# The opening of a two-layer decoder trunk on one core: loading the input ahead of the first weights, and reordering the first gate's products

## The chip, the core and the metric

The kernel runs on one core of one Trainium2 chip. The metric is the device time of one execution in microseconds (us). Four engines matter here: TensorE (PE, with its weight loads PEld beside it), VectorE (DVE), ScalarE (ACT) and GpSimd (POOL). SyncE (SP) issues nearly all transfers from memory.

## The reference

Two layers, each of a half-step SwiGLU block, a mixer of three attention groups, and another half-step SwiGLU block. The input x is 256 tokens by 1024 features, in float32; a SwiGLU block has 2816 hidden columns. What the change touches is the very first norm and the first gate and up products:

```python
def rms_norm(x, g):
    y = x * rsqrt(mean(x * x, axis=-1, keepdims=True) + 1e-6)
    return y * g

def swiglu(x, w_gate, w_up, w_down):
    return (silu(x @ w_gate) * (x @ w_up)) @ w_down

h = x
for l in range(2):
    h = h + 0.5 * swiglu(rms_norm(h, ffn1_norm[l]), ffn1_w_gate[l], ffn1_w_up[l], ffn1_w_down[l])
    h = h + hybrid_mixer(rms_norm(h, mix_norm[l]), ...)
    h = h + 0.5 * swiglu(rms_norm(h, ffn2_norm[l]), ffn2_w_gate[l], ffn2_w_up[l], ffn2_w_down[l])
```

## The kernel before

**Products in three parts.** Every float32 operand that goes through TensorE is split into a high part, rounded to the format that TensorE takes at full speed, and a low part, the residual. A product is then high x high plus high x low plus low x high. A weight tile `raw` of 1024 columns a partition (8 blocks of 128 rows by 128 output columns) is copied to `wh` (the class `Weights`, method `high`, L117, on ACT) and its residual goes to `wl` (method `low`, L121, on DVE). The normed input lies in one tile `xhl` whose two halves are the high part `norm.h` and the low part `norm.l`, side by side for each of its 8 blocks. So one **wide** product, 512 columns, multiplies `wh` with both halves at once, and one **narrow** product, 256 columns, adds `wl` times the high half. `proj` does eight wide and eight narrow products for one tile of 128 hidden columns.

**The norm.** x is loaded into `trunk` with tokens on the partitions. `Norm.turn` (L329) turns two blocks of it with four TensorE transposes into a PSUM bank of the tag `acc`. `Norm.high` (L318, ACT) scales a block by the norm's gain `gT` and writes the high part; `Norm.low` (L321, DVE) writes the residual. The division by the root mean square comes later, on the hidden values. The gains arrive as rows and are turned by `turn_gains` (L177 on TensorE, copied by DVE, L178).

**Order.** Nothing reorders instructions: each engine runs them as the program writes them down. Transfers go through SP's queue in the order of the calls. The first two weight tiles are loaded by hand in pieces: raw 0 holds the first two gate tiles (its first tile in two pieces of 256 KB, its second as one of 512 KB), raw 1 the first two up tiles (512 KB each). Until now the queue begins: x quarter 0, first half of the first gate tile, x quarter 1, second half of that tile, x quarters 2 and 3, the first up tile, the second gate tile, the second up tile. On ACT's own queue the identity matrix and the gains are loaded.

**The opening.** TensorE does seven products of ones (`WARM`), the transposes of x's quarter 0, the gains' transpose, and seven more products of ones. Then it goes through x by quarters: for the first gate tile it does three narrow products a block (`wh` with the high half, `wl` with the high half, `wh` with the low half), 24 in all, with the next quarters' transposes between them. The first gate tile is split by halves: `wh` by ACT (L1118) and `wl` by POOL (L1119). Only then does `ffn` run `proj` for the first up tile (`u0`), the second gate tile (`g1`), the second up tile (`u1`) and so on; in the first block the tiles g0, u0, g1, u1 stand in four PSUM banks of the tag `gu`. The squares for the mean (L344) follow on ACT, and their sum and root are formed during g1 and u1.

## Time and profile before

| | |
|---|---|
| median of 3 runs | 1041.45 us (1041.19 to 1041.46) |
| the profiled execution | 1041.75 us, with a span of 1039.8 us on the core |
| TensorE busy | 1034.6 us, granted clock 1.00 |
| DVE, ACT, POOL busy | 808.5, 594.9, 142.7 us |
| bytes moved | 181.70 MB, 175 GB/s on average |

In the lines of the profile an instruction group is named by its line in the kernel (L294 is the one line through which all products go), its engine, what it writes and reads, its shape and its count. In a timeline the first number is the start in us from the span's beginning and the second the time to the end of the group; a bracket tells how long the engine stood idle before it and what released it. A waits row gives the total, the count and the longest. A windows row gives a stretch, its length, the busy time of PE, PEld, DVE, ACT and POOL, the granted clock, the DMA engines' busy share and their GB/s. An issue row of a transfer ends with its size and the time from issue to landing.

### The profile page before, as it was taken

Reading aid. Unit: us, or ns where it says so; the run is one execution under the profiler, and the core shown is the slowest. Engines: PE = TensorE matmul, PEld = TensorE weight load, DVE = VectorE, ACT = ScalarE, POOL = GpSimd, SP = SyncE. Lnnn points to the kernel's source line nnn. Section 1 sums busy time; section 2 is a strip of 40 time slices with the busy share of each in tenths; the row PEclk is TensorE's granted clock in tenths of the full one; section 3 lists DMA queues with packets and bytes.
Section 4 is the critical chain, followed back from the end, with each engine's and each line's share of the span. In section 5 each row is a group of like instructions: output and inputs, shape, how many; then the busy total and the mean of one; then the engine's idle time right before and its main releaser. Section 6 shows DMA issues by size and latency. Waiting matters only on the chain.

```text
span 1039.8 us, 15145 instructions
## 1 busy us (share of the span) xinstructions
PE 1034.6 (100%) x5659; PEld 899.4 (86%) x5659; DVE 808.5 (78%) x1536; ACT 594.9 (57%) x1047; POOL 142.7 (14%) x173
## 2 busy tenths in 40 slices
PE   9999999999999999999999999999999999999998
PEld 8888888898888888888888888888988888888887
DVE  4997777789876887777788777777898768877775
ACT  6565555667754655555466555547667556555551
POOL 1003000167700000000000200002765000000000
PEclk9999999999999999999999999999999999999999
DMA  9675555555431374654646464555455214564631
GB/s 322 218 245 181 189 207 171 175 187 185 154 130 42 122 242 161 204 193 172 202 163 215 159 240 158 207 171 185 163 193 173 81 61 160 184 237 147 223 122 41
DMA packets 130905, 181.70 MB, mean 175 GB/s; under 512 B 7008, under 2 KB 104720, under 8 KB 130832
## 3 DMA queue, kind: packets, MB, share of 16 engines
q1 hardware_dynamic: 130656, 180.65, 51.0%
q8 instruction: 45, 0.74, 0.3%
q14 instruction: 28, 0.23, 0.1%
q10 hardware_dynamic: 176, 0.07, 0.0%
HBM read 179.67 MB, written 1.05 MB: 174 GB/s over the span
## 4 chain that ended last, share of the span: by engine, by line
PE 99%; DMA 1%; ACT 0%; SPq 0%; DVE 0%; issue 0%
PE ps_gu L294 66%; PE ps_acc L294 30%; PE ps_acc L329 1%; PE ps_gu L948 1%; PE ps_gu L1050 1%; DMA trunk<-in_x_dram 1%; PE ps_acc L649 0%; PE ps_acc L948 0%; PE ps_gu L981 0%; ACT wh L117 0%; SPq L91 0%; SPq L188 0%; PE ps_acc L355 0%; PE ps_acc L981 0%; DVE tmp L435 0%; DVE trunk L368 0%
## 5 line engine op out<-in xcount | busy, mean ns | idle before, releaser
L121 DVE TENSOR_TENSOR wl<-raw,wh 128x1024 fp32r<-128x1024 f32 (+2 forms) x343 | 416.6, 1220 | 29.2 <-ACT wh L117 29.0
L117 ACT CAST wh<-raw 128x1024 fp32r<-128x1024 f32 (+2 forms) x343 | 345.7, 1036 | 5.4 <-PE ps_gu L294 4.8
L294 PE MATMUL ps_gu<-xhl,wh 128*128 128x512 f32 (+1 forms) x1408 | 335.2, 389 | 0.2 <-DVE tmp L435 0.2
L294 PEld LDWEIGHTS ps_gu<-xhl,wh 128*128 128x128 f32 x1408 | 261.7, 188 | 53.2 <-DVE tmp L435 0.4
L294 PEld LDWEIGHTS ps_gu<-xhl,wl 128*128 128x128 f32 x1400 | 180.7, 191 | 7.2
L294 PE MATMUL ps_gu<-xhl,wl 128*128 128x256 f32 x1400 | 184.5, 283 | 0.0
L294 PE MATMUL ps_gu<-wh,xhl 128*128 128x512 f32 (+2 forms) x512 | 158.5, 379 | 0.0
L435 DVE TENSOR_TENSOR tmp<-ps_gu,tmp 128x256 f32<-128x256 f32 x175 | 72.5, 423 | 107.4 <-ACT tmp L434 107.2
L294 PE MATMUL ps_acc<-wh,hh 128*128 128x512 f32 (+1 forms) x352 | 137.7, 391 | 0.0
L294 PE MATMUL ps_acc<-wl,hh 128*128 128x512 f32 (+1 forms) x352 | 137.5, 391 | 0.0
L294 PE MATMUL ps_acc<-wh,hl 128*128 128x512 f32 (+1 forms) x352 | 136.5, 388 | 0.0
L434 ACT COPY tmp<-ps_gu 128x256 f32<-128x256 f32 x175 | 63.1, 371 | 93.9 <-PE ps_gu L294 93.8
L294 PEld LDWEIGHTS ps_gu<-wh,xhl 128*128 128x128 f32 x512 | 94.8, 188 | 14.5
L449 ACT CAST hh<-tmp 128x256 fp32r<-128x256 f32 x80 | 32.6, 407 | 119.9 <-DVE tmp L446 119.9
L294 PE MATMUL ps_gu<-wl,xhl 128*128 128x512 f32 (+2 forms) x256 | 95.7, 374 | 0.0
L305 POOL TENSOR_TENSOR y_n<-msq,minus_half 128x2 f32<-128x2 f32 x6 | 7.7, 1281 | 539.9 <-DVE msq L304 539.9
L441 ACT ACTIVATE tmp<-tmp 128x256 f32<-128x256 f32 x88 | 36.9, 419 | 77.8 <-DVE tmp L439 77.4
L294 PEld LDWEIGHTS ps_acc<-wh,hl 128*128 128x128 f32 x352 | 66.1, 188 | 14.0
L294 PEld LDWEIGHTS ps_acc<-wh,hh 128*128 128x128 f32 x352 | 66.4, 189 | 11.7
L294 PEld LDWEIGHTS ps_acc<-wl,hh 128*128 128x128 f32 x352 | 66.4, 189 | 11.4 <-DVE wl L121 0.7
L294 PEld LDWEIGHTS ps_gu<-wl,xhl 128*128 128x128 f32 x256 | 48.2, 188 | 6.6
L318 ACT ACTIVATE xhl<-ps_acc,gT 128x256 fp32r<-128x256 f32 x48 | 19.1, 475 | 37.2 <-PE ps_acc L329 37.1
(221 smaller groups left out, 1013.7 us busy)
## 6 DMA issues: line engine op xcount, KB each, us to landing
raw<-in_ffn_w_down_dram SPq DMA_DIRECT2D x44, 1024.0 KB, 4.9
raw<-in_ffn_w_gate_dram SPq DMA_DIRECT2D x43, 1024.0 KB, 6.7
raw<-in_ffn_w_up_dram SPq DMA_DIRECT2D x43, 1024.0 KB, 7.4
raw<-in_w_in_dram SPq DMA_DIRECT2D x24, 1024.0 KB, 5.0
raw<-in_w_out_dram SPq DMA_DIRECT2D x8, 1024.0 KB, 4.8
raw<-in_w_in_dram SPq DMA_DIRECT2D x4, 768.0 KB, 4.7
raw<-in_w_in_dram SPq DMA_DIRECT2D x4, 656.0 KB, 5.2
trunk<-in_x_dram SPq DMA_DIRECT2D x4, 256.0 KB, 4.7
```

What stands on the lines that cost most here:

```text
L117: self.nc.scalar.copy(hv, src)
L121: (engine or self.nc.vector).tensor_tensor(lv, self.srcs[self.n_low], hv.bitcast(F32), op=ALU.subtract)
L294: T.matmul(o, l, r, start=start, stop=stop, skip_group_check=True)
L305: G.tensor_tensor(y, dst, minus_half[:, :n], op=ALU.pow)
L318: A.activation(self.h[:, m], src, AF.Copy, scale=gT[:, self.col + m:self.col + m + 1])
L329: T.transpose(ps[:, i, t * P:(t + 1) * P], trunk[:, t, (2 * mp + i) * P:(2 * mp + i + 1) * P], ident)
L434: A.copy(o, ps[:, 1])
L435: V.tensor_tensor(o, ps[:, 0], o, op=ALU.add)
L441: A.activation(th, t_, AF.Tanh, scale=0.5)
L449: (V.tensor_copy if late else A.copy)(hh, t_)
L948: T.transpose(b[:, j * P:(j + 1) * P], pj[i][:, j * P:(j + 1) * P], ident)
L1050: T.transpose(b[:66, i * S + t * P:i * S + (t + 1) * P], src[t][:, 2 * hp_ + i, :], ident)
```

## The change

It has five parts, all in the opening:

- SP's queue begins with x: quarters 0 and 1, then quarters 2 and 3 as one transfer of 512 KB. The two halves of the first gate tile follow, then the first up tile as before.
- The gains are turned ahead of x's quarter 0 on TensorE. x's quarters are turned one after the other, with 2, 3, 0 and 4 products of ones behind them; no gate product stands between them.
- On ACT, six of x's eight blocks come ahead of the first half of the gate tile, two behind it. The second half of the gate tile's `wh` is copied by DVE, behind six of the eight residuals of x.
- The first gate tile is done with wide products, like all other tiles: eight wide ones, then the first up tile's eight wide ones, then the gate's eight narrow ones and the up's eight narrow ones.
- `ffn` takes over both banks, `g0` and `u0`, and starts with g1.

From g1 on, every engine's instructions stand in the same order as before.

```diff
-    def load_x(mp):
-        cols = slice(256 * mp, 256 * mp + 256)
+    def load_x(mp, n=1):
+        cols = slice(256 * mp, 256 * (mp + n))
...
-    for mp in range(1, 4):
-        if mp < 3:
-            W.load(0, mp - 1)
-        load_x(mp)
+    load_x(1)
+    load_x(2, 2)
+    W.load(0, 0)
+    W.load(0, 1)
     W.load(1, 0)
     W.load(0, 2)
     W.load(1, 1)
...
-        first = g0 is not None
         early = {}
         if first:
-            u0 = proj()
+            g0, u0 = first
             g1 = proj(norm.sums, 6)
...
-    g0 = bank("gu").rearrange("p (a b) -> p a b", a=2)
+    first = [bank("gu").rearrange("p (a b) -> p a b", a=2) for _ in range(2)]
     xT = []
 
-    def turn_x(mp):
-        xT.append(norm.turn(mp))
-
-    def gate(w, xs, ks):
-        for k in ks:
-            mm(g0[:, int(xs is norm.l)], w[:, k], xs[:, k], w is wh and xs is norm.h and k == 0,
-               xs is norm.l and k == KT - 1)
+    def warm_up(n):
+        for i in range(n):
+            mm(warm[:, P:2 * P], ones, ones, False, i == n - 1)
...
-    def split_gate(hf):
+    def split_gate(hf, copy):
         ks = slice(4 * hf, 4 * hf + 4)
-        A.copy(wh[:, ks], src[:, ks])
+        copy(wh[:, ks], src[:, ks])
         G.tensor_tensor(wl[:, ks], src[:, ks], wh[:, ks].bitcast(F32), op=ALU.subtract)
 
-    turn_x(0)
     turn_gains(0)
-    for i in range(WARM):
-        mm(warm[:, P:2 * P], ones, ones, False, i == WARM - 1)
-    split_gate(0)
-    first_norm(0)
-    turn_x(1)
-    split_gate(1)
-    for mp in range(4):
-        ks = range(2 * mp, 2 * mp + 2)
-        gate(wh, norm.h, ks)
-        if mp < 2:
-            turn_x(mp + 2)
-        if mp > 0:
-            gate(wl, norm.h, range(4) if mp == 1 else ks)
-        gate(wh, norm.l, ks)
-        if mp < 3:
-            first_norm(mp + 1)
+    for mp, n in enumerate((2, 3, 0, 4)):
+        xT.append(norm.turn(mp))
+        warm_up(n)
+    for mp in range(3):
+        first_norm(mp)
+    split_gate(0, A.copy)
+    split_gate(1, V.tensor_copy)
+    first_norm(3)
     W.low_done()
-    W.take()
+    ws = [W.take()]
     W.high()
     W.low()
     W.high()
     W.low()
+    ws.append(W.take())
+    for w, ps in zip(ws, first):
+        for k in range(KT):
+            mm(ps, w[0][:, k], norm.x[:, k], k == 0, False)
+    for w, ps in zip(ws, first):
+        for k in range(KT):
+            mm(ps[:, 0], w[1][:, k], norm.h[:, k], False, k == KT - 1)
```

More of the change, by code (lines that the diff above doesn't have):

```diff
@@ L369, in residual, with ffn @@
         return d
-    def ffn(norm, nxt, aside=None, g0=None):
+    def ffn(norm, nxt, aside=None, first=None):
         hid = {}
@@ L1150 @@
     for l in range(DEPTH):
-        norm = ffn(norm, lambda: Norm(1, l), lambda: before_mixer(l), g0 if l == 0 else None)
+        norm = ffn(norm, lambda: Norm(1, l), lambda: before_mixer(l), first if l == 0 else None)
         norm = mixer(l, norm, lambda: Norm(2, l))
```

## The prediction

> **What bounds the kernel now.** I read the page first, then TensorE's waits, then one long window.

> ```profile
> span 1039.8 us, 15145 instructions
> PE 1034.6 (100%) x5659; PEld 899.4 (86%) x5659; DVE 808.5 (78%) x1536; ACT 594.9 (57%) x1047; POOL 142.7 (14%) x173
> ```
> ```profile
> PE ps_gu L294 <- POOL minus_half L183: 1.0, 1, 1.0
> PE ps_acc L329 <- DMA trunk<-in_x_dram: 0.8, 1, 0.8
> PE ps_gu L294 <- DVE tmp L435: 0.2, 1, 0.2
> ```
> ```profile
> 14.64:1039.80 1025.16, 1021.78 (x5576) 887.43 (x5574) 802.32 (x1525) 585.19 (x1029) 139.38 (x158) 1.00 0.51 173
> ```

> TensorE is busy 1034.6 of 1039.8 us, and the waits list names only three stalls of it in the whole run. The third fence is the window from 14.64 us to the end: 1021.78 of 1025.16 us busy at a granted clock of 1.00. There is no slack behind 14.64 us in which a late or early start could vanish, and no instruction there changes kind or order. So the change is worth what it does to one moment: the start of the second gate's products, g1, at 14.64 us. Only the opening has to be worked out.

> ```profile
> 2.63 1.63 PE L294 MATMUL ps_gu<-ones 128*128 128x128 f32 x7
> 4.91 1.83 PE L294 MATMUL ps_gu<-ones 128*128 128x128 f32 x14
> 6.57 0.60 PE L329 MATMUL ps_acc<-cst,trunk 128*128 128x128 f32 x4
> 6.93 0.48 PE L294 MATMUL ps_gu<-xhl,wh 128*128 128x256 f32 x2
> 8.21 0.66 PE L329 MATMUL ps_acc<-cst,trunk 128*128 128x128 f32 x4 [0.80 <-DMA trunk<-in_x_dram]
> 8.62 0.72 PE L294 MATMUL ps_gu<-xhl,wh 128*128 128x256 f32 x4
> 11.54 2.31 PE L294 MATMUL ps_gu<-xhl,wh 128*128 128x256 f32 x10
> 13.69 1.11 PE L294 MATMUL ps_gu<-xhl,wl 128*128 128x256 f32 x8
> 14.64 2.00 PE L294 MATMUL ps_gu<-xhl,wh 128*128 128x512 f32 x8
> 16.48 1.11 PE L294 MATMUL ps_gu<-xhl,wl 128*128 128x256 f32 x8
> 17.43 2.00 PE L294 MATMUL ps_gu<-xhl,wh 128*128 128x512 f32 x8
> ```
> ```profile
> 5.43 0.83 ACT L318 ACTIVATE xhl<-ps_acc,gT 128x256 fp32r<-128x256 f32 x2
> 7.51 0.62 ACT L1118 CAST wh<-raw 128x512 fp32r<-128x512 f32 x1 [1.25 <-DMA raw<-in_ffn_w_gate_dram]
> 8.03 2.63 ACT L318 ACTIVATE xhl<-ps_acc,gT 128x256 fp32r<-128x256 f32 x6
> 10.55 1.05 ACT L117 CAST wh<-raw 128x1024 fp32r<-128x1024 f32 x1
> 11.90 1.05 ACT L117 CAST wh<-raw 128x1024 fp32r<-128x1024 f32 x1 [0.30 <-DMA raw<-in_ffn_w_gate_dram]
> ```
> ```profile
> 5.02 0.17 DVE L178 COPY gT<-ps_gu 128x16 f32<-128x16 f32 x1 [5.02 <-PE ps_gu L177]
> 8.90 2.67 DVE L321 SCALAR_TENSOR_TENSOR xhl<-ps_acc,gT,xhl 128x256 fp32r<-128x256 f32 x6 [1.73 <-PE ps_acc L329]
> 11.63 2.58 DVE L121 TENSOR_TENSOR wl<-raw,wh 128x1024 fp32r<-128x1024 f32 x2
> 8.20 1.29 POOL L1119 TENSOR_TENSOR wl<-raw,wh 128x512 fp32r<-128x512 f32 x1 [1.32 <-ACT wh L1118]
> ```

> Durations overlap in the pipe, so I use starts. Eight wide products (512 columns) take 16.48 - 14.64 = 1.84 us, 0.23 each; eight narrow ones (256 columns) 17.43 - 16.48 = 0.95 us, 0.119 each. The row of ten at 11.54 holds the gate's last two narrow products and the first up's eight wide ones, so the up's wide products start at 11.54 + 0.24 = 11.78 and its narrow ones at 13.69. ACT's steps by starts: one activation of x (10.55 - 8.03) / 6 = 0.42, half a gate tile 0.52, a whole tile 1.05.

> **What arrives when.** Landings are issue plus the last column of the issue rows; the last two rows are windows, which end with the DMA engines' share and GB/s:

> ```profile
> 1.18 0.45 ACTq L173 DMA_DIRECT2D tmp<-in_ffn_norm_dram  x1
> tmp<-in_ffn_norm_dram ACTq DMA_DIRECT2D x1, 8.0 KB, 3.0
> 3.86 0.47 SPq L91 DMA_DIRECT2D raw<-in_ffn_w_up_dram  x1
> raw<-in_ffn_w_up_dram SPq DMA_DIRECT2D x1, 512.0 KB, 6.4
> 2.79 1.02 SPq L188 DMA_DIRECT2D trunk<-in_x_dram  x2
> trunk<-in_x_dram SPq DMA_DIRECT2D x1, 256.0 KB, 5.5
> 5.00:6.25 1.25, 1.25 (x12) 1.25 (x13) 0.17 (x1) 1.25 (x3) 0.65 (x1) 1.00 0.73 220
> 6.75:10.25 3.50, 2.70 (x24) 2.49 (x23) 1.76 (x6) 2.63 (x7) 1.42 (x2) 1.00 1.13 356
> ```

> The first up's weights land at 3.86 + 6.4 = 10.26 us. In front of them stand 1 MB of x and two gate pieces, before and after alike: the change only permutes them. The engines already move 356 GB/s (share 1.13) from 6.75 to 10.25 us, so the permutation brings the up no earlier, except for a dip to 220 GB/s from 5.00 to 6.25 us. The dip costs 1.25 x (1 - 220/356) = 0.48 us. It falls on the second gate piece, whose landing ACT awaited until 7.51; whether it belongs to that piece or to that time no row says.

> **The change part by part.**

> Transfers. Count SP's queue in pieces of 256 KB: today x, gate, x, gate, x, x, then the up; afterwards four of x (the half counts as two), two of the gate, then the up. The last of x takes the fourth place, the second gate piece's of today. So all of x is in at about 7.5 us, where today its third quarter ends TensorE's wait at 8.21. The gate pieces land where x's last two quarters do now. With the dip gone the half lands at 7.0.

> Norm scales ahead of x. TensorE's queue now holds the scales' transpose in front of x's first quarter, and all behind it waits for 1.18 + 3.0 = 4.18 us, when the scales land. The warm-up products end there anyway (the last seven start at 2.63 and go by the 0.23 us pace of 1.63 / 7). The cost is one small transpose, about 0.1 to 0.2 us on the first quarter. It is hidden: ACT's four activations for the first two quarters then run from about 5.1 to 6.9, and x's half is not readable before 8.17. The cover is 1.2 us; without it the whole delay would reach the up's cast.

> x as it lands. Turning the half starts at 7.5 and its first pair is readable 0.66 us later, at 8.17 (the row at 8.21). ACT: two activations to 9.01, the gate's first half to 9.53, two activations to 10.37, then the up's cast. That cast is the step that decides: it needs ACT free (10.37) and the weights (10.26), so 10.37 to 11.42, and TensorE can start the up's wide products at about 11.47.

> The gate's second half goes from ACT to DVE. This copy is not in the trace of before. Its bounds are DVE's smallest copy, 0.17 (the row at 5.02), and DVE's two-operand step on twice the size, 1.29 (2.58 / 2). I take half of the latter, 0.65, since the size is half and ACT's 0.52 for the same tile lies near it. It stands in DVE's queue after six residual steps (0.445 each, 2.67 / 6) and before the last two. With activations ready at 8.59 and 9.01, DVE is through the sixth at 9.5, the copy at 10.15, and the last two at 11.05. TensorE's gate products start at about 9.6 and the eighth waits until 11.05, so they end at 11.3, just ahead of 11.47. Here the cover is thin: at 1.29 us for the copy they end at 11.92 and the sum grows by 0.45; at 0.17 it gains nothing, since the cast still ends at 11.42.

> POOL's two residual halves (1.29 each) now start at 9.55 and end by 12.2. The gate's narrow products need them only at 13.3, so they cost nothing.

> The order of the products. Today 24 narrow gate products are spread over x's arrival. Afterwards there are eight wide and eight narrow, 1.84 + 0.95 = 2.79 us against 24 x 0.119 = 2.86: the work itself is equal within 0.1. What moves is the place: the eight narrow ones, 0.95 us, go behind the up's wide products, where they are on the path. Ahead of those, TensorE only waits.

> The sum: up's wide 11.47 to 13.31, two sets of narrow ones 1.90, g1 at 15.21 instead of 14.64, so 0.57 us later. Break-even is a start of the up's wide products at 14.64 - 3.74 = 10.90, that is, a cast begun at 9.8. If the dip is gone ahead of x, the half lands at 7.0 and ACT is free at 9.9, with the up in at 9.78; the start is 11.0 and the loss 0.1. Between 0.1 and 0.57, I take 0.5, because the rows as they stand give the upper end and only an unproved shift of the dip gives the lower.

> Behind g1 nothing waits longer: its weights are cast from 11.90 (landing) and split on DVE to about 14.3, and their narrow products start at 17; the squares and the later casts follow the landing at 11.90, not TensorE.

> The profiled execution took 1041.75 us for its span of 1039.8, and the median of the runs is 1041.45, 0.30 less. So 1041.75 + 0.5 - 0.30 = 1041.95, given as 1042.0. A measurement of this kernel can tell about 0.2%, 2.08 us, from no change; the forecast is no change, on the slow side.

> **The clock, weighed.** The first warm-up records pace at 0.23 us, those from 4.91 at (6.57 - 4.91) / 14 = 0.119: TensorE starts at half pace and doubles near 4.2 us, though the granted clock reads 1.00. Before's longest stretch without an ordinary product, after the two at 6.93 until 8.62, costs nothing of that. [...]

> **The rivals.**

> [...]

> Slower by less: the x half does not land in the fourth place but as late as the last quarter does now, the second of the pair issued from 2.79, so 2.79 + 0.51 + 5.5 = 8.8. ACT is then free 1.3 us later, and g1 is 1.9 us late: 1043.3.

> Level or a little faster: the dip belongs to the second gate piece alone, so x lands before it, at 6.9 or earlier, and ACT comes to the up's cast at 9.8, as its weights land. Then g1 starts at 14.6: 1041.4. For it: the dip is one short stretch, and the gate's first piece, of the same shape, came ahead of it.

> Faster by over 0.2% would need g1 at 12.56, so the up's cast begun at 7.7, when its weights land at 10.26. Only something outside the opening could do that.

> **How the numbers follow.** Chances: forecast (0.3 to 0.8 us late) 0.58; level 0.20; late half 0.08; clock 0.08; outside the opening 0.06, half each way. The first two alone reach from 1041.2 to 1042.3; with the runs' spread and part of the late half I give 1041.0 to 1043.0, which leaves out the clock, the rest of the late half and the outside cases, some 0.18. Faster by over 0.2% 0.03; slower 0.08 for the clock, 0.03 from outside and none of the late half, which stays just within, so 0.11; the same 0.86.

> **What would show it.** In the profile after: the scales' transpose near 4.3; x's half turned from 7.0 to 7.5; the up's cast on ACT begun at 9.9 to 10.4; the up's wide products at 11.0 to 11.5 after a wait for ACT; 16 narrow products in a row; g1 at 14.7 to 15.2. I am wrong if the half is turned before 6.7 or after 8.2, if the wide products pace at 0.46, or if the window behind g1 is not again 1025.2 us.

## The result, and the profile after

The changed kernel takes 1043.64 us in the median of 15 runs (1042.95 to 1045.5), the kernel before 1041.85 beside it. The ratio is 1.0022, 95% interval 1.0015 to 1.0029: 1.8 us slower by the medians and 2.3 by the ratio (1.6 to 3.0), outside the stated range of 1041.0 to 1043.0. Two executions far above all others, one of before (2633.5 us) and one of no_ones (1279.56), are left out below. The changed kernel's times do not lie around one value, so that a median of them can jump by over a microsecond with a single run. With six more runs of it below, nine of 21 lie at 1042.95 to 1043.64 (median 1043.16) and twelve at 1044.73 to 1045.5 (median 1044.95), with none between. The first trace, at 1045.28 us, is of the upper group.

The page, TensorE's waits and the window from the second gate's products to the end, of the changed kernel:

```profile
span 1043.4 us, 15138 instructions
PE 1037.6 (99%) x5655; PEld 901.7 (86%) x5655; DVE 810.4 (78%) x1537; ACT 594.2 (57%) x1046; POOL 143.1 (14%) x173
```
```profile
PE ps_gu L294 <- POOL minus_half L183: 1.0, 1, 1.0
PE ps_gu L177 <- DMA tmp<-in_ffn_norm_dram: 0.8, 1, 0.8
PE ps_gu L294 <- DVE wh L1113: 0.4, 1, 0.4
PE ps_gu L294 <- DVE tmp L435: 0.2, 1, 0.2
```
```profile
18.13:1043.40 1025.27, 1021.86 (x5576) 887.68 (x5574) 802.17 (x1525) 582.90 (x1024) 139.73 (x158) 1.00 0.51 172
```

The window behind g1 is 1025.27 us, against 1025.16 before. So the whole loss is the start of g1: 18.13 instead of 14.64, 3.49 us, and the two profiled executions differ by 1045.28 - 1041.75 = 3.53. TensorE's idle time hardly grew: two new waits, 0.8 and 0.4 us, while the old one of 0.8 for x is gone. Most of the loss is hidden as busy time, 1037.6 instead of 1034.6 us for nearly the same work. It shows in the timeline of TensorE's opening:

```profile
5.16 0.26 PE L177 MATMUL ps_gu<-cst,tmp 16*128 16x16 f32 x1 [0.83 <-DMA tmp<-in_ffn_norm_dram]
5.35 1.11 PE L329 MATMUL ps_acc<-cst,trunk 128*128 128x128 f32 x4
6.25 1.06 PE L294 MATMUL ps_gu<-ones 128*128 128x128 f32 x4
7.11 1.06 PE L329 MATMUL ps_acc<-cst,trunk 128*128 128x128 f32 x4
7.96 1.49 PE L294 MATMUL ps_gu<-ones 128*128 128x128 f32 x6
9.24 1.30 PE L329 MATMUL ps_acc<-cst,trunk 128*128 128x128 f32 x8
10.38 1.06 PE L294 MATMUL ps_gu<-ones 128*128 128x128 f32 x8
11.54 1.21 PE L294 MATMUL ps_gu<-xhl,wh 128*128 128x512 f32 x4
13.20 3.18 PE L294 MATMUL ps_gu<-xhl,wh 128*128 128x512 f32 x12 [0.44 <-DVE wh L1113]
18.13 2.00 PE L294 MATMUL ps_gu<-xhl,wh 128*128 128x512 f32 x8
```

Read the starts; a product of ones leaves two records. From 5.35 four transposes take 6.25 - 5.35 = 0.90 us, four records of ones 0.86, six more 1.28: 0.21 each, the half pace at which the kernel begins, and it lasts into the row at 9.24. Before, the same records went at 0.119 from 4.91 on. Meanwhile the data lay ready, as the issue rows show (the half is issued at about 1.7):

```profile
tmp<-in_ffn_norm_dram ACTq DMA_DIRECT2D x1, 8.0 KB, 3.8
trunk<-in_x_dram SPq DMA_DIRECT2D x1, 512.0 KB, 4.6
3.29 0.52 SPq L91 DMA_DIRECT2D raw<-in_ffn_w_up_dram  x1
raw<-in_ffn_w_up_dram SPq DMA_DIRECT2D x1, 512.0 KB, 6.1
```

The half of x was in at 6.3 and the up's weights at 9.4, both earlier than forecast. But TensorE's queue came to the half only at 9.24. The scales, issued at 1.20, landed at 5.0 instead of 4.18. Then the copy that went to DVE, beside GpSimd:

```profile
11.57 1.29 POOL L1114 TENSOR_TENSOR wl<-raw,wh 128x512 fp32r<-128x512 f32 x1 [10.27 <-ACT wh L1113]
11.81 1.33 DVE L1113 CAST wh<-raw 128x512 fp32r<-128x512 f32 x1
```

It took 1.33 us, not 0.65, and TensorE's fifth gate product waited for it until 13.20.

### The profile page after: what moved, and what is told of

Same layout as the page of the kernel before. It is cut to its first block, busy times and chain, and to the rows that moved or that the text cites. A ratio compares the mean times of both kernels' runs of the same rounds, so it can differ in the third digit from the quotient of the medians.

```text
span 1043.4 us, 15138 instructions
## 1 busy us (share of the span) xinstructions
PE 1037.6 (99%) x5655; PEld 901.7 (86%) x5655; DVE 810.4 (78%) x1537; ACT 594.2 (57%) x1046; POOL 143.1 (14%) x173
## 3 DMA queue, kind: packets, MB, share of 16 engines
HBM read 179.67 MB, written 1.05 MB: 173 GB/s over the span
## 4 chain that ended last, share of the span: by engine, by line
PE 99%; DMA 0%; ACT 0%; DVE 0%; issue 0%; ACTq 0%
PE ps_gu L294 66%; PE ps_acc L294 30%; PE ps_acc L329 1%; PE ps_gu L947 1%; PE ps_gu L1049 1%; DMA tmp<-in_ffn_norm_dram 0%; PE ps_acc L648 0%; PE ps_acc L947 0%; PE ps_gu L980 0%; ACT wh L117 0%; DVE wh L1113 0%; PE ps_acc L355 0%; PE ps_acc L980 0%; ACT xhl L318 0%; DVE xhl L321 0%
## 5 line engine op out<-in xcount | busy, mean ns | idle before, releaser
L121 DVE TENSOR_TENSOR wl<-raw,wh 128x1024 fp32r<-128x1024 f32 (+2 forms) x343 | 417.3, 1223 | 30.0 <-ACT wh L117 30.0
L117 ACT CAST wh<-raw 128x1024 fp32r<-128x1024 f32 (+2 forms) x343 | 345.6, 1037 | 4.8 <-PE ps_gu L294 4.8
L294 PE MATMUL ps_gu<-xhl,wh 128*128 128x512 f32 x1400 | 334.8, 390 | 0.7 <-DVE wh L1113 0.4
L294 PEld LDWEIGHTS ps_gu<-xhl,wh 128*128 128x128 f32 x1400 | 260.9, 188 | 54.7 <-DVE wh L1113 0.9
L294 PEld LDWEIGHTS ps_gu<-xhl,wl 128*128 128x128 f32 x1400 | 180.5, 191 | 7.2
L294 PE MATMUL ps_gu<-xhl,wl 128*128 128x256 f32 x1400 | 184.0, 283 | 0.0
L294 PE MATMUL ps_gu<-wh,xhl 128*128 128x512 f32 (+2 forms) x512 | 158.6, 379 | 0.0
L435 DVE TENSOR_TENSOR tmp<-ps_gu,tmp 128x256 f32<-128x256 f32 x175 | 72.6, 424 | 107.1 <-ACT tmp L434 106.8
L294 PE MATMUL ps_acc<-wh,hh 128*128 128x512 f32 (+1 forms) x352 | 137.8, 392 | 0.0
L294 PE MATMUL ps_acc<-wl,hh 128*128 128x512 f32 (+1 forms) x352 | 137.6, 391 | 0.0
L294 PE MATMUL ps_acc<-wh,hl 128*128 128x512 f32 (+1 forms) x352 | 136.6, 388 | 0.0
L294 PEld LDWEIGHTS ps_gu<-wh,xhl 128*128 128x128 f32 x512 | 94.8, 188 | 14.5
L294 PE MATMUL ps_gu<-wl,xhl 128*128 128x512 f32 (+2 forms) x256 | 95.8, 374 | 0.0
L294 PEld LDWEIGHTS ps_acc<-wh,hl 128*128 128x128 f32 x352 | 66.2, 188 | 14.0
L294 PEld LDWEIGHTS ps_acc<-wh,hh 128*128 128x128 f32 x352 | 66.4, 189 | 11.7
L294 PEld LDWEIGHTS ps_acc<-wl,hh 128*128 128x128 f32 x352 | 66.4, 189 | 11.4 <-DVE wl L121 0.7
L294 PEld LDWEIGHTS ps_gu<-wl,xhl 128*128 128x128 f32 x256 | 48.3, 189 | 6.6
L318 ACT ACTIVATE xhl<-ps_acc,gT 128x256 fp32r<-128x256 f32 x48 | 19.1, 475 | 42.3 <-PE ps_acc L329 42.3
## 6 DMA issues: line engine op xcount, KB each, us to landing
raw<-in_ffn_w_up_dram SPq DMA_DIRECT2D x2, 512.0 KB, 6.0
```

The costliest lines, as they stand in the source:

```text
L117: self.nc.scalar.copy(hv, src)
L121: (engine or self.nc.vector).tensor_tensor(lv, self.srcs[self.n_low], hv.bitcast(F32), op=ALU.subtract)
L294: T.matmul(o, l, r, start=start, stop=stop, skip_group_check=True)
L318: A.activation(self.h[:, m], src, AF.Copy, scale=gT[:, self.col + m:self.col + m + 1])
L435: V.tensor_tensor(o, ps[:, 0], o, op=ALU.add)
```

## The experiments

Theory **clock**: TensorE does not come to full pace by 4.3 us, because its queue stands at the scales, and it then works through transposes and products of ones at half pace. Theory **copy**: DVE's copy waits for GpSimd. Theory **order**: the narrow products behind the up's wide ones cost 0.95 us, as the prediction had it. The time of each profiled execution follows its g1 start by the constant tail, so g1 starts are compared beside the times. The ratios are against the kernel before, run beside each; its medians there were 1041.5 to 1041.8.

**again**: the changed kernel, unaltered.

> The changed kernel itself, unaltered, for a second trace. Its fifteen times lie in two groups, about 1043.0 to 1043.6 and 1044.7 to 1045.5, and the trace at hand (1045.28) is of the upper one. Theory clock: the scales landed at 5.1 us, TensorE stood idle 0.83 us and stayed at half pace to about 9.7; a run of the lower group would show TensorE at full pace earlier. If this trace is near 1043.2, x's half is turned before 9.2 us and the transposes of the half pace at about 0.11, not 0.21. Rival, copy and order alone: the pace is the same in both groups and the difference lies elsewhere.

Median 1044.85 of 6 runs, ratio 1.0031 (1.0018 to 1.0043); the profiled execution fell in the lower group, at 1043.16. TensorE's timeline:

```profile
4.36 0.26 PE L177 MATMUL ps_gu<-cst,tmp 16*128 16x16 f32 x1
4.54 0.77 PE L329 MATMUL ps_acc<-cst,trunk 128*128 128x128 f32 x4
5.15 0.61 PE L294 MATMUL ps_gu<-ones 128*128 128x128 f32 x4
7.33 1.09 PE L329 MATMUL ps_acc<-cst,trunk 128*128 128x128 f32 x8 [0.46 <-DMA trunk<-in_x_dram]
9.42 1.21 PE L294 MATMUL ps_gu<-xhl,wh 128*128 128x512 f32 x4
11.08 3.20 PE L294 MATMUL ps_gu<-xhl,wh 128*128 128x512 f32 x12 [0.44 <-DVE wh L1113]
16.02 2.00 PE L294 MATMUL ps_gu<-xhl,wh 128*128 128x512 f32 x8
```

Here the scales came in time, the four records at 5.15 took 5.60 - 5.15 = 0.45 (full pace), and x's half was turned when it landed, at 7.33. The g1 start is 16.02, 2.11 us before the other trace's; the medians of the groups lie 1.8 apart. The wait for DVE's copy stays.

**gains_behind**: the scales' transpose one step later.

```diff
-    turn_gains(0)
     for mp, n in enumerate((2, 3, 0, 4)):
         xT.append(norm.turn(mp))
         warm_up(n)
+        if mp == 0:
+            turn_gains(0)
```

> Only the scales' transpose moves, from ahead of x's first quarter to behind it and its two products of ones. Theory clock: no idle stretch at 4.3, so TensorE goes to full pace at 4.2 to 4.6, x's half is turned by about 7.5, the second gate's products start near 15.0 to 15.7 (18.1 in the trace of the change) and the time is 1042.0 to 1042.6. Rival, the copy on DVE and the order of the products carry the loss: the time stays at 1043.2 to 1045.2.

1042.82 (1042.40 to 1043.69, 11 runs), ratio 1.0011 (1.0002 to 1.0020). The upper group is gone: none of 11 times, where twelve of 21 lay in it. The median is 0.2 above the end of the forecast. In the trace the first transposes still go at half pace, the rest at full, and g1 starts at 15.76, just past the 15.7 that was expected:

```profile
4.36 1.08 PE L329 MATMUL ps_acc<-cst,trunk 128*128 128x128 f32 x4
5.24 0.65 PE L294 MATMUL ps_gu<-ones 128*128 128x128 f32 x4
9.17 1.20 PE L294 MATMUL ps_gu<-xhl,wh 128*128 128x512 f32 x4
10.83 3.18 PE L294 MATMUL ps_gu<-xhl,wh 128*128 128x512 f32 x12 [0.46 <-DVE wh L1113]
```

**warm_long**: the scales stay ahead, the wait is filled.

```diff
-    for i in range(WARM):
-        mm(warm[:, :P], ones, ones, i == 0, i == WARM - 1)
+    for i in range(WARM + 4):
+        mm(warm[:, :P], ones, ones, i == 0, i == WARM + 3)
```

> Eleven products of ones ahead of the scales' transpose instead of seven, nothing else. Theory clock: the eight more records bridge the wait for the scales, TensorE turns to full pace near 4.3 and the scales are turned at about 5.3; the second gate's products start near 15.2 to 15.8, the time is 1042.2 to 1042.8. Rival, late scales alone (their wait, not the pace): no gain, since nothing lands earlier, 1043.2 to 1045.2. Rival, copy and order: likewise no gain.

1043.88 (1043.26 to 1044.29, 11 runs), ratio 1.0019 (1.0010 to 1.0027). One group again. The median misses theory clock's forecast by 1.1 us and lies where the rival, late scales alone, allowed it. The trace (1043.79) tells them apart: the scales are turned at 5.79, later than in the first trace (5.16), and yet everything behind them goes at full pace and g1 starts at 16.63 instead of 18.13. So the longer start does secure the pace; the added products take the place of the wait, and that costs the gain.

**warm_short**: the opposite, three products at the start (`WARM - 4`).

> The changed kernel with three products of ones at its start instead of seven, nothing else; TensorE then stands idle from about 2.3 us until the scales land. Theory clock: the lower group of the change's times goes, every run is at half pace until 9 to 10 us and lies at 1044.6 to 1045.6. Rival, late scales without the clock: nothing lands later, so two groups as before, with runs near 1043.2.

1045.08 (1044.19 to 1045.24, 5 runs), ratio 1.0033 (1.0021 to 1.0046). Four of the five lie in the upper group and none in the lower; the profiled one, the lowest, shows half pace into the row at 7.59, where the first trace had it into the row at 9.24:

```profile
4.79 0.25 PE L177 MATMUL ps_gu<-cst,tmp 16*128 16x16 f32 x1 [2.16 <-DMA tmp<-in_ffn_norm_dram]
6.74 1.06 PE L329 MATMUL ps_acc<-cst,trunk 128*128 128x128 f32 x4
7.59 1.06 PE L294 MATMUL ps_gu<-ones 128*128 128x128 f32 x6
```

No transfer was touched, and the lower group is missing; late scales alone would have left it. But five runs are few: with nine of 21 in the lower group, five in a row would miss it about one time in sixteen.

**before_gains**: this part alone in the kernel before.

```diff
-    turn_x(0)
     turn_gains(0)
+    turn_x(0)
```

> The kernel before, with one part of the change alone: the scales' transpose ahead of x's first quarter. Theory clock: TensorE stands idle from 4.3 until the scales land (4.2 to 5.2); in the runs where it is not at full pace by then, the seven products of ones behind it take 3.0 us instead of 1.66 and all of the opening slips, so two groups of times appear, one at 1041.5 to 1042.2 and one 1.5 to 3 us above it. Rival, late scales without the clock: one group, 0 to 0.5 above before, since x's third quarter at 8.2 still sets the pace.

1042.37 (1041.72 to 1044.0, 11 runs), ratio 1.0008 (0.9999 to 1.0016): not clear of before. Nine times lie at 1041.7 to 1042.6 and two at 1043.66 and 1044.0. The trace (1042.35) shows half pace into the products of ones, 14 records in 7.79 - 5.58 = 2.21 us instead of 1.66, and g1 starts at 15.01, 0.37 late. TensorE waited only 0.15 us for the scales there, so this trace does not test what a long wait costs in that opening. The upper group is rarer than forecast, and of the 33 runs of before beside it one reaches 1043.74 as well.

```profile
4.67 1.11 PE L329 MATMUL ps_acc<-cst,trunk 128*128 128x128 f32 x4
5.58 2.38 PE L294 MATMUL ps_gu<-ones 128*128 128x128 f32 x14
7.79 0.60 PE L329 MATMUL ps_acc<-cst,trunk 128*128 128x128 f32 x4
```

**pool_swap**: in the changed kernel, GpSimd does the second half's residual first, so that it has nothing to do while DVE copies.

```diff
     split_gate(0, A.copy)
     split_gate(1, V.tensor_copy)
+    gate_low(1)
+    gate_low(0)
```

`gate_low` is the `G.tensor_tensor` line, taken out of `split_gate`.

> GpSimd takes the two residual halves of the first gate tile in the other order, so that it stands idle while DVE copies the second half (1.33 us in the trace of the change, beside GpSimd's 1.29 us on the first half). [...] Rival: the copy takes 1.3 us by itself, and the time stays within 0.2 of the change. Theory clock says nothing on it: the half pace until 9.7 stays, and so do two groups of times.

1042.88 (1042.29 to 1045.03, 11 runs), ratio 1.0016 (1.0007 to 1.0025). Both groups are there: six times at 1042.29 to 1042.88 (median 1042.71, 0.45 under the changed kernel's lower group), one at 1043.69, four at 1044.62 to 1045.03. In the trace TensorE waits 0.91 us for the scales, as long as in the first trace, but goes at full pace behind them, and the gate's first product starts at 9.44 (9.42 in again, 11.54 in the first trace). So such a wait by itself need not cost anything; the half pace behind it does. DVE's and GpSimd's rows:

```profile
9.70 0.42 DVE L1113 CAST wh<-raw 128x512 fp32r<-128x512 f32 x1
10.20 3.53 POOL L1117 TENSOR_TENSOR wl<-raw,wh 128x512 fp32r<-128x512 f32 x2 [8.90 <-DVE wh L1113]
11.11 3.70 DVE L121 TENSOR_TENSOR wl<-raw,wh 128x1024 fp32r<-128x1024 f32 x2
```

The copy takes 0.42 us by itself. From the gate's first product to the up's first wide one it is 11.50 - 9.44 = 2.06 us, and in again, with the copy at 1.34, 12.27 - 9.42 = 2.85. But the slowing does not vanish, it moves: GpSimd's two residuals, 1.29 each before, now take 3.53 together, and DVE's two of the whole tile 3.70 instead of 2.58. TensorE's first narrow product waits 0.31 for GpSimd, so the g1 start, 15.79, is 0.23 ahead of again's, less than the 0.44 for which TensorE waited there for the copy.

**gb_act_copy**: gains_behind, with `split_gate(1, A.copy)`.

> The kernel gains_behind, with the gate tile's second half copied by ACT, right behind the first, instead of by DVE. Theory copy: DVE's copy beside GpSimd (1.25 us in gains_behind) is the step that holds the gate's fifth product to 10.83; with ACT's 0.52 instead, the fifth follows the fourth, the up's wide products start at about 11.4 and the second gate's products at 15.1 to 15.4 (15.76 in gains_behind): 1042.1 to 1042.5. Rival, the order of the products: the copy is hidden and the time stays at 1042.8.

1042.79 (1042.29 to 1043.37, 11 runs), ratio 1.0011 (1.0002 to 1.0020). The trace is as forecast: no wait for the copy, g1 at 15.16, 1042.29. But that execution is the fastest of eleven, and the median is that of gains_behind. Of the 0.60 us between the two traces 0.33 is an earlier start of the gate (8.84 instead of 9.17); the copy itself gives 0.27, and the times do not show it.

**gb_order**: gains_behind, with the products in the order of all later tiles, the gate's narrow ones ahead of the up's wide ones.

```diff
     for w, ps in zip(ws, first):
         for k in range(KT):
             mm(ps, w[0][:, k], norm.x[:, k], k == 0, False)
-    for w, ps in zip(ws, first):
         for k in range(KT):
             mm(ps[:, 0], w[1][:, k], norm.h[:, k], False, k == KT - 1)
```

> The kernel gains_behind, with the gate's eight narrow products ahead of the up's wide ones again. The prediction's step says that the narrow products cost 0.95 us by standing behind: then the second gate's products start near 14.9 and the time falls to about 1041.9. Theory work: TensorE has the same products to do after the gate's fifth product in either order and waits for nothing there, so nothing moves (15.5 to 15.8, 1042.5 to 1042.8); a wait for GpSimd's second half at 12.15 could even add 0.1 to 0.3.

1043.11 (1042.83 to 1043.43, 11 runs), ratio 1.0013 (1.0004 to 1.0022), against 1042.82. The forecast that follows from the prediction's step, 1041.9, is off by over a microsecond.

```profile
11.17 1.34 PE L294 MATMUL ps_gu<-xhl,wh 128*128 128x512 f32 x4 [0.45 <-DVE wh L1113]
12.35 1.11 PE L294 MATMUL ps_gu<-xhl,wl 128*128 128x256 f32 x8
13.30 2.00 PE L294 MATMUL ps_gu<-xhl,wh 128*128 128x512 f32 x8
16.09 1.09 PE L294 MATMUL ps_gu<-xhl,wh 128*128 128x512 f32 x4
```

From the fifth gate product to g1 it is 16.09 - 11.17 = 4.92 us, and in gains_behind 15.76 - 10.83 = 4.93. Once TensorE has the data it runs through, and the order within that stretch is worth nothing; what counts is when the stretch begins. The whole stretch from the gate's first product to g1 is as steady: 6.58 to 6.60 us in the six traces with DVE's copy beside GpSimd (the first one, again, gains_behind, warm_long, warm_short, gb_order), and 6.32 to 6.35 in pool_swap, gb_act_copy, no_ones and gb_act_loads. All other differences of g1 lie ahead of the gate.

**no_ones**: gb_act_copy without the nine products of ones between x's quarters.

> The kernel gb_act_copy without the nine products of ones between x's quarters. If they stand on the path: x's half is turned as it lands (6.3 to 7.2) and the second gate's products start 0.1 to 0.4 earlier than 15.16: 1042.4 to 1042.7. [...]

Seven times lie at 1042.32 to 1042.61 and three at 1043.57 to 1044.58; ratio 1.0013 (1.0004 to 1.0022). Of the trace (1042.61):

```profile
5.16 0.66 PE L329 MATMUL ps_acc<-cst,trunk 128*128 128x128 f32 x4
7.17 1.09 PE L329 MATMUL ps_acc<-cst,trunk 128*128 128x128 f32 x8 [1.36 <-DMA trunk<-in_x_dram]
9.26 4.59 PE L294 MATMUL ps_gu<-xhl,wh 128*128 128x512 f32 x16 [1.00 <-ACT wh L1113]
```

In this trace TensorE idles 1.36 and 1.00 us, and the eight transposes (1.09 us in all) and all products behind (16 narrow ones in 1.90 us) still go at full pace; g1 starts at 15.59, later than expected, as x's half came late. So the wait for x's half need not cost the pace even without the products of ones. The three upper times have no trace, but their granted clock is 0.998, 0.998 and 0.996, and none of the other executions of these experiments shows less than 0.999. By estimate, a share of 0.002 of 1040 us is what about 4 us at half the clock would take away. That would fit a pace that fell back; no trace shows such a fall, and where in the run it would lie is open.

**gb_act_loads**: gb_act_copy with the loads interleaved as before.

> The kernel gb_act_copy with the loads in the old order again (quarters of x between the gate's pieces). By the rows of before, x's third quarter lands at 8.2 and the last at 8.8; ACT ends its fifth and sixth block at 9.7 instead of 8.2, and the second gate's products start at 16.2 to 16.5: 1043.5 to 1044.1, 1.0 to 1.3 above gb_act_copy. Rival, the up's weights set the end: they land no later than before, so the time stays at 1042.8 within 0.3.

1043.20 (1043.14 to 1043.83, 11 runs), ratio 1.0016 (1.0007 to 1.0025): 0.4 above gb_act_copy by the medians, less than forecast, with ratios whose intervals overlap. In its trace TensorE hardly waits ahead of the gate, and yet the half pace lasts to about 7; g1 starts at 16.17. Seven of gb_act_copy's eleven times lie below the lowest here, so x first is probably worth having in the new program.

**before_xfirst**: before, with the new order of the loads alone.

> The kernel before with one part of the change alone, the order of the loads (x's quarters 0 and 1 and its half, then the gate's pieces). ACT's queue, unchanged, begins with the gate's first half, which now lands at 7.1 instead of 4.9: all its steps follow it, the up's cast ends at 12.6 instead of 11.6, and the second gate's products start near 15.5: 1042.3 to 1042.8. Rival: x's third quarter was the wait (8.2), it lands at 6.3 to 7.2 now, and the time falls to 1041.0 to 1041.4.

1043.19 (1042.28 to 1043.74, 11 runs), ratio 1.0016 (1.0008 to 1.0025), worse than forecast. ACT's row and TensorE's wait for it:

```profile
8.03 0.62 ACT L1118 CAST wh<-raw 128x512 fp32r<-128x512 f32 x1 [4.71 <-DMA raw<-in_ffn_w_gate_dram]
9.08 0.76 PE L294 MATMUL ps_gu<-xhl,wh 128*128 128x256 f32 x2 [0.93 <-ACT xhl L318]
```

ACT's queue begins with the gate's first half, which now lands at 8.0 instead of 4.9, and x waits behind it.

**early_copies**: gains_behind's loads, the scales directly behind x's first quarter, both gate halves copied by ACT behind x's first four blocks, no ones behind x's half, and the gate's products by halves.

> A version that may beat both: loads as in the change, scales turned behind x's first quarter, both halves of the gate tile copied by ACT behind x's first four blocks and ahead of its last four, no products of ones after x's half, the gate's products by halves (four wide, four narrow, twice) ahead of the up's. By the rows of gains_behind: ACT is through the last block at about 10.1 and the up's cast at 11.2, the gate is done near 11.3, the second gate's products start at 14.0 to 14.6 (14.64 before): 1041.2 to 1041.8. Rival: the up's weights land at 10.3 to 10.8 and set the end: 14.6 to 15.2, 1041.8 to 1042.4.

1042.54 (1042.17 to 1043.48, 11 runs), ratio 1.0008 (0.9999 to 1.0017), g1 at 15.13. The forecast was 1041.2 to 1041.8. It beats the changed kernel, and not the one before. DVE gives the reason: its last four residuals start only at 9.77, because ACT's four activations now stand behind two copies, and the gate's products end at 12.35.

```profile
9.77 1.66 DVE L321 SCALAR_TENSOR_TENSOR xhl<-ps_acc,gT,xhl 128x256 fp32r<-128x256 f32 x4 [1.49 <-ACT xhl L318]
```

## Why the prediction was wrong

**What bounds the kernel**: right. In every trace the span is the g1 start plus 1025.2 to 1025.3 us, and the loss is set by the opening alone.

**Transfers**: right in kind. x's half landed at 6.3 and about 7.2 in the two traces of the changed kernel, where 7.0 to 7.5 was forecast. The up's weights landed at 9.4 and 10.8, around the 10.26 that was used.

**Norm scales ahead of x**: this step failed first. It took 4.18 us from one landing and set it equal to the end of the products of ones, so that the scales cost nothing but 0.1 to 0.2 us under a cover of 1.2. The landing moves: 4.2, 5.0 and 5.1 us in again, the first trace and pool_swap. A wait of 0.83 us at that point can put off the pace, and the half pace then doubles the price of everything that the change had put between x and the gate. From the scales' transpose to the gate's first product it was 11.54 - 5.16 = 6.38 us in the first trace, and with the same wait but full pace, in pool_swap, 9.44 - 5.22 = 4.22.

When does the pace come up? The trace files keep the granted clock as records, and a windows row prints 1.00 also where none stands. The first record begins where the starts show the doubling: at 4.07 us in before, 4.17 in pool_swap, 4.83 in again, 7.12 in gb_act_loads and 9.77 in the first trace. In all fourteen traces this record ends within 2 us of the span's end and lasts 1034.24 or 1037.65 us. The two lengths differ by 3.41 us and are 303 and 304 times that, as if the clock could change only on a grid of 3.41 us. So look at the 3.41 us ahead of each record, and at the 3.41 us ahead of those (behind the stretch and its length stands TensorE's busy time):

```profile
0.76:4.17 3.41, 3.19 (x14) 3.06 (x14) 0.00 (x0) 1.59 (x2) 0.55 (x9) 1.00 0.56 157
```
```profile
2.94:6.36 3.42, 2.59 (x13) 2.28 (x13) 0.17 (x1) 0.38 (x2) 0.00 (x0) 1.00 1.04 349
6.36:9.77 3.41, 3.41 (x18) 3.41 (x18) 1.57 (x4) 1.68 (x4) 0.00 (x0) 1.00 1.15 346
```
```profile
0.29:3.71 3.42, 2.73 (x13) 2.73 (x14) 0.00 (x0) 1.59 (x2) 0.72 (x13) 1.00 0.40 130
3.71:7.12 3.41, 3.41 (x17) 3.15 (x17) 0.17 (x1) 0.62 (x2) 0.00 (x0) 1.00 0.99 306
```

The first row is pool_swap, the next two the first trace, the last two gb_act_loads. In each of the fourteen traces the pace doubled at the end of the first such stretch in which TensorE was busy for 0.87 of it or more; the stretches before were busy for 0.80 or less. In pool_swap a stretch ended at 4.17, just ahead of the wait from 4.31, and the wait did no harm. In the first trace the wait lay inside the stretch from 2.94 to 6.36, which was busy for only 0.76, and the pace came one stretch later. In gb_act_loads no wait was to blame: TensorE's first product, at 0.98, came too late for the stretch that began at 0.29. Nor do the stretches start with the kernel: counted back in steps of 3.41 us from the first record, the first whole one begins 0.66 us after its start in before, 0.76 in pool_swap, 0.29 in gb_act_loads and 2.94 in the first trace. Where the kernel's start falls between two of them would then, as the author estimates from these four, decide which group an execution lands in. That the upper group's other executions are of this kind rests on one trace of it and on gains_behind and warm_long, where the group is gone.

The prediction gave the clock a chance of 0.08 and named wide products at 0.46 us as a sign against its forecast. No run shows that term: in the first trace the gate's wide products ran at 0.23 to 0.24 where nothing held them up. The half pace fell on the transposes and products of ones ahead of them, and it had not fallen back but had not yet ended. The transposes counted as TensorE's work in that: without them the stretch from 3.71 to 7.12 in gb_act_loads would be busy for 0.57, less than the 0.80 of the one before, which did not suffice.

**The copy on DVE**: mis-sized. 0.65 was taken, 1.25 to 1.34 was measured beside GpSimd and 0.42 without it. The bound of 1.29 was drawn for the copy's own length, and its price of 0.45 was named and then not taken. In the first trace GpSimd's residual ends at 11.57 + 1.29 = 12.86, and the copy that started at 11.81 ends 0.28 us after that, as if it had waited. Why the two slow each other no run shows. What removing it is worth is less clear: 0.79 us up to the up's first wide product in pool_swap, about 0.26 at g1, 0.45 in the lower group's times with pool_swap and nothing visible with gb_act_copy.

**The order of the products**: wrong as a step, though the sum hid it. gb_order shows that the 0.95 us are not a cost of their place. The prediction's 3.74 us from the up's first wide product to g1 held (16.02 - 12.27 = 3.75 in again) because TensorE runs through from there in any order.

**The sum**: it had g1 at 15.21, and the lower group's trace has it at 16.02, 0.81 later. The gate began at 9.42, as forecast (9.6). The copy ended at 11.03 instead of 10.15 and the last residuals at 11.81 instead of 11.05, so the up's wide products started at 12.27 instead of 11.47: 0.80 us, nearly the whole difference. The up's cast, which the prediction took as the deciding step, was over at 11.87. The upper group's further 2.1 us are the pace. In time the lower group (1043.16) lies 1.2 above the forecast of 1042.0: 0.8 by g1, and most of the rest because the forecast took 1041.45 for the kernel before, where 15 runs gave 1041.85.

What stays open: with the scales behind x and the copy on ACT, the median is still 1.1 us above that of before, while the trace (g1 at 15.16) accounts for 0.5. That trace is the fastest of eleven runs, and its clock record begins the earliest of all, at 3.96. How much of the rest is pace in the runs that were not traced is not settled.

## What to carry to other kernels

In an opening, cover every wait ahead of the first dense work with TensorE work until the pace is up, and do not put a small, late load at the head of its queue: where a wait of under a microsecond fell into the wrong stretch, it cost two. Here the pace came up between 4 and 7.1 us after the kernel's start where TensorE hardly waited, and at 8.0 and 9.8 where it had waited ahead of that. A busy share of 99% says nothing of this, so compare the starts of equal instructions in the two traces. When a copy moves to DVE, look at what GpSimd does at that moment: here the same copy took 0.42 us without it and 1.25 to 1.34 beside it.
